# Tables of a state-space mixer set up in one batch, shorter norms, and two mixers' tails issued together, in a two-layer hybrid-head block

## The chip, the core and the metric

The kernel runs on one core of one Trainium2 chip. The metric is device time in microseconds of one execution; three runs are known, with a median of 4328.35 us (4321.64 to 4334.05). Lower is better.

## The reference, cut to what matters

Two layers act on 1024 latent tokens and 256 context tokens of width 1024, all in float32. Each layer modulates a norm, projects it, feeds four mixers of 256 channels each (gated linear attention, S5, Mamba2/SSD, latent attention), projects their outputs back and ends with a squared-ReLU MLP.

```python
def _modulate(h, g, shift, scale):
    return _rms(h, g) * (1.0 + scale) + shift

def s5_mixer(u_ctx, u_lat, a_re, a_im, log_step, b_re, b_im, c_re, c_im, d_skip, w_glu, b_glu):
    lam = lax.complex(a_re, a_im)
    lam_bar = jnp.exp(lam * jnp.exp(log_step)[..., None])
    b_bar = ((lam_bar - 1.0) / lam)[..., None] * lax.complex(b_re, b_im)
    ...
    h = scan(h -> lam_bar * h + b_bar u)        # forwards and backwards, 16 groups of 64 states
    y = real(c h) + d_skip * u
    y = gelu(y);  return y * sigmoid(y @ w_glu + b_glu)

for l in range(2):
    m = split(silu(c) @ w_mod[l] + b_mod[l], 6)
    a = _modulate(h, norm1_g[l], m[0], m[1]) @ w_in[l]
    ya, yb, yc, yd = gdn_mixer(a0), s5_mixer(a1), mamba2_mixer(a2), mla_mixer(a3)
    h = h + m[2] * (concat(ya, yb, yc, yd) @ w_out[l])
    h = h + m[5] * (relu(_modulate(h, norm2_g[l], m[3], m[4]) @ w_ff1[l])**2 @ w_ff2[l])
```

The S5 mixer needs tables of powers of `lam_bar` (magnitude, sine and cosine) for its chunks, which depend on the weights alone; the kernel makes them for both directions and 16 groups in each layer.

## The kernel before, in words

Tokens stand in three blocks of columns: block 0 (256 context tokens), blocks 1 and 2 (512 latent tokens each), always worked in the order 2, 0, 1, with features on the partitions. Every large product is made of three fp32r matmuls, high times high, low times high and high times low, so that each operand exists as a `hi` and a `lo` part: `a_hi` and `a_lo` for a normed block, `w_hi` and `w_lo` for a weight, `f_rh` and `f_rl` inside the ffn. The kernel is one list of instructions per engine: a scheduler written by hand (`Streams`) runs generators side by side by a virtual time, and each stage has a share (`SHARE`, line 147) that says how much virtual time its work costs. The list that comes out decides the order on each engine and on SP's DMA queue; nothing is reordered at run time.

The stages, by `main` (line 1823), with their times in the profile of before:

- Start, 0 to 69 us: the three blocks of `h` are loaded; `norm_scale` makes each block's scale (squares on ACT, sums `n_sq` and `n_acc` on DVE, a column sum on PE in `g`, `rsqrt` into `n_rr`, and a broadcast on PE that ACT copies to `n_acc`); `mod_pe` makes the first modulation vectors `md` and from them the gain `gs`; the stream `s5_tables` starts.
- Norms and the first part of the input projection to 325 us, its second part to about 650. `norm` (line 1633) makes for each of 8 pieces of 128 features `n_x`, then `a_hi` on ACT, then `n_x` once more and the difference `a_lo`. `norm_next` and `norm_all` chain the blocks: one starts when the one before is done.
- The mixers to 1310 us: SSD and latent attention (`mla`, names beginning with `m_`) in the main stream, and beside it the stream `beside`: linear attention (`gdn`, names beginning with `g_`), then S5 (names beginning with `5_`). S5 loads its parameters (`5_sd`, `5_wg`), its inputs (`5_U`), the block matrices `5_TZ` and 8 factor tables `5_fc`, does a recurrence, and ends with `s5_out`: gelu into `5_yf`, a gate product on PE, `5_mo`, and a store to the mixers' buffer `mx`.
- The output projection to 1404, the second norms, the ffn of layer 0 to 2440 us. Beside the ffn run layer 1's modulation vectors and from about 1870 us layer 1's S5 tables.
- Layer 1 in the same way: norms from 2404, mixers to 3474, second norms 3552 to 3625, ffn to 4309.

`s5_tables` (line 1205) calls `s5_setup` four times (two directions, two halves of 8 groups); each takes an exponential of the step, two exponentials of magnitude, and sines and cosines for 17 exponents (forms of 128x136). After each setup it calls `s5_products` four times: `5_t_hh` and `5_t_k` go through PE at once, then the co and si factors follow on DVE and POOL, and the result `5_fc` is stored to `s5d`. Both uses of `rsqrt` (line 268) are a bit trick and four Newton steps of four DVE instructions each. The inner part of `norm` reads

```python
x = self.t(wk, [128, 512], F32, "n_x", bufs=2)
nc.vector.tensor_tensor(x[:, :w], h[:, k], rb[:, :w], op=OP.mult)
nc.scalar.activation(hi[:, k], x[:, :w], AF.Identity, bias=sh, scale=gs)
```

and after it the second `n_x` is made in place, on ACT for odd pieces and on DVE for even ones; `a_lo` is on DVE for pieces 3 and 7 and on POOL for the other six. In `beside` the linear attention is finished, with its gating and its output stores (`outp`), before S5 begins.

## Time and profile before

| what | value |
|---|---|
| median of three runs | 4328.35 us (4321.64 to 4334.05) |
| the profiled execution, its own time | 4310.99 us |
| its span on the core | 4309.2 us |
| mean granted TensorE clock | 0.931 of full |
| PE busy | 3817.7 us, 89% of the span |
| DVE busy | 2716.2 us, 63% |
| POOL busy | 1455.5 us, 34% |
| ACT busy | 1259.1 us, 29% |
| DMA moved | 367.29 MB, 85 GB/s over the span |

The profile is of one execution. An engine is busy where one of its instructions ran; idle time is put down to what released the instruction behind it. In the rows all instructions carry line 125, a helper that issues them, so they are told apart by their tiles: `out<-in`, with an engine, an operation and a form. Names of tiles are those of the sections above; `mm`, `g`, `x`, `m` and `c` are accumulators in PSUM.

### The profile page before, as it was taken

How to read it: one execution, taken by the hardware profiler on the slowest of the kernel's cores; microseconds unless marked ns; L12 is line 12 of the kernel's file. 1: busy time of each engine (PE TensorE's matmuls, PEld its weight loads, DVE VectorE, ACT ScalarE, POOL GpSimd, SP SyncE). 2: the span in 40 equal slices, each digit the busy share in tenths (PEclk: the TensorE clock that was granted, in tenths of full speed). 3: DMA queues.
4: the chain of work that ended last, by engine and by line, in shares of the span. 5: the costliest groups of instructions: out<-in, count | busy, mean ns of one | idle time of the engine just before them, and what ended most of it. 6: DMA issues, size and time to landing. Idle time of an engine off the chain costs nothing.

```text
span 4309.2 us, 61386 instructions
## 1 busy us (share of the span) xinstructions
PE 3817.7 (89%) x23280; PEld 3058.1 (71%) x23280; DVE 2716.2 (63%) x6419; ACT 1259.1 (29%) x2015; POOL 1455.5 (34%) x1664
## 2 busy tenths in 40 slices
PE   5789897789978899999999798997959988999999
PEld 2567776667656688887788677775846676888887
DVE  7966567775644799997775645567765536444443
ACT  3324434333312411121222343244322323222121
POOL 3532533454451211133332224435435433222121
PEclk7899998789999999999999899998969999999999
DMA  5347520100345033311111243342041231111111
GB/s 184 125 159 221 194 98 32 45 2 5 74 123 176 30 98 98 103 60 55 50 62 62 81 136 100 106 144 76 14 106 52 58 135 32 57 40 59 40 59 59
DMA packets 170872, 367.29 MB, mean 85 GB/s; under 512 B 46160, under 2 KB 88400, under 8 KB 166864
## 3 DMA queue, kind: packets, MB, share of 16 engines
q1 hardware_dynamic: 170576, 363.37, 26.2%
q8 instruction: 183, 3.00, 0.3%
q14 instruction: 113, 0.93, 0.1%
HBM read 277.42 MB, written 85.89 MB: 84 GB/s over the span
## 4 chain that ended last, share of the span: by engine, by line
PE 46%; DVE 15%; POOL 3%; DMA 2%; ACT 2%; issue 2%; SPq 0%; DVEq 0%; ACTq 0%; POOLq 0%
PE mm L125 38%; PE m L125 3%; DVE mod_acc L125 3%; PE g L125 2%; PE c L125 2%; DVE h L125 2%; DVE n_x L125 1%; PE x L125 1%; DVE s_ca L125 1%; POOL a_lo L125 1%; POOL g_pr L125 1%; DVE g_scr L125 1%; DVE rsq_u L125 1%; SPq L125 0%; DVE f_r L125 0%
## 5 line engine op out<-in xcount | busy, mean ns | idle before, releaser
L125 PE MATMUL mm<-a_hi,w_hi 128*128 128x512 f32 (+1 forms) x2576 | 978.2, 381 | 45.5 <-ACT st L125 28.6
L125 PE MATMUL mm<-a_lo,w_hi 128*128 128x512 f32 (+1 forms) x2576 | 971.4, 378 | 38.0 <-POOL a_lo L125 18.5
L125 PE MATMUL mm<-a_hi,w_lo 128*128 128x512 f32 (+1 forms) x2576 | 965.8, 375 | 2.4 <-DVE w_lo L125 2.4
L125 POOL TENSOR_TENSOR w_lo<-w_raw,w_hi 128x1024 fp32r<-128x1024 f32 x189 | 465.0, 2469 | 1270.9 <-ACT w_hi L125 1268.9
L125 DVE SCALAR_TENSOR_TENSOR h<-mm,md,h 128x512 f32<-128x512 f32 (+1 forms) x680 | 467.4, 693 | 250.7 <-PE mm L125 246.9
L125 PEld LDWEIGHTS mm<-a_hi,w_hi 128*128 128x128 f32 x2576 | 499.1, 194 | 141.9 <-ACT st L125 32.6
L125 PEld LDWEIGHTS mm<-a_lo,w_hi 128*128 128x128 f32 x2576 | 500.4, 194 | 131.0 <-POOL a_lo L125 30.5
L125 PEld LDWEIGHTS mm<-a_hi,w_lo 128*128 128x128 f32 x2576 | 499.3, 194 | 83.9 <-DVE w_lo L125 2.9
L125 PE MATMUL mm<-f_rh,w_hi 128*128 128x512 f32 (+1 forms) x1280 | 478.3, 374 | 27.8 <-DVE f_r L125 13.7
L125 PE MATMUL mm<-f_rl,w_hi 128*128 128x512 f32 (+1 forms) x1280 | 473.6, 370 | 0.0
L125 PE MATMUL mm<-f_rh,w_lo 128*128 128x512 f32 (+1 forms) x1280 | 473.1, 370 | 0.0
L125 ACT CAST w_hi<-w_raw 128x1024 fp32r<-128x1024 f32 x234 | 242.2, 1048 | 735.5 <-PE mm L125 600.5
L125 DVE SCALAR_TENSOR_TENSOR f_r<-mm,f_r 128x512 f32<-128x512 f32 (+1 forms) x160 | 101.5, 634 | 360.1 <-ACT f_rh L125 359.4
L125 PEld LDWEIGHTS mm<-f_rh,w_hi 128*128 128x128 f32 x1280 | 243.7, 190 | 72.0 <-DVE h L125 16.5
L125 PEld LDWEIGHTS mm<-f_rh,w_lo 128*128 128x128 f32 x1280 | 243.1, 190 | 40.5
L125 PEld LDWEIGHTS mm<-f_rl,w_hi 128*128 128x128 f32 x1280 | 243.5, 190 | 39.1
L125 ACT ACTIVATE f_r<-mm 128x512 f32<-128x512 f32 (+1 forms) x160 | 88.1, 551 | 547.7 <-PE mm L125 474.0
L125 DVE SCALAR_TENSOR_TENSOR mod_acc<-mod_w,cond,mod_acc 128x128 f32<-128x128 f32 x672 | 240.4, 404 | 1.4
L125 POOL TENSOR_TENSOR m_sum<-m_sum,m_p 128x512 f32<-128x512 f32 x128 | 164.1, 1282 | 124.0 <-ACT m_p L125 117.9
L125 DVE SCALAR_TENSOR_TENSOR s_ca<-s_cx,s_prm,s_ca 128x255 f32<-128x255 f32 (+2 forms) x240 | 148.7, 644 | 24.4 <-ACT s_ca L125 22.1
L125 POOL TENSOR_TENSOR a_lo<-n_x,a_hi 128x512 fp32r<-128x512 f32 (+1 forms) x66 | 77.8, 1188 | 154.4 <-DVE n_x L125 139.5
L125 DVE TENSOR_TENSOR f_rl<-f_r,f_rh 128x512 fp32r<-128x512 f32 (+1 forms) x160 | 116.1, 726 | 2.0
(493 smaller groups left out, 6629.0 us busy)
## 6 DMA issues: line engine op xcount, KB each, us to landing
w_raw<-in_w_ff SPq DMA_DIRECT2D x128, 512.0 KB, 3.6
w_raw<-in_w_in SPq DMA_DIRECT2D x90, 512.0 KB, 3.9
mod_w<-in_w_mod SPq DMA_DIRECT2D x80, 512.0 KB, 3.7
pd<-st SPq DMA_DIRECT2D x80, 257.0 KB, 2.3
s5d<-5_fc SPq DMA_DIRECT2D x32, 577.0 KB, 2.8
5_fc<-s5d SPq DMA_DIRECT2D x16, 1154.0 KB, 6.3
g_cx<-pd SPq DMA_DIRECT2D x18, 643.0 KB, 4.9
h<-in_hT SPq DMA_DIRECT2D x4, 2048.0 KB, 9.9
```

The costliest lines, as they stand in the source:

```text
L125: return f(*args, **kw)
```

## The change

The first part batches the tables. A new `s5_small` makes the step's exponential, `xd`, `th`, the reduced angles `ph`, `rho` and the reciprocal `den` once for all 32 columns (16 groups, 2 directions); `s5_setup` takes its 8 columns of them. Sines, cosines and magnitudes are made for 9 exponents in place of 17 (forms of 128x72), and `s5_products` reads them reversed where it read the other 8. Its PE part goes behind the co and si factors, and its second operand has a buffer of its own, `5_t_o`. `5_prm` is loaded by 4 DMAs instead of 16, and the copy of `rho` goes from DVE to ACT. In the whole program DVE goes from 6421 to 5862 instructions, ACT from 2017 to 2048, POOL from 1669 to 1647, SP from 1023 to 1011; PE keeps 18658.

The second part shortens `rsqrt` to three Newton steps of three instructions (12 instead of 19 in all) and `norm` to a multiply by `gs` and the scale in one instruction. In 8 pieces DVE has 12 instructions of one kind where it had 8, 4 and 2 of three kinds; ACT keeps 12 and POOL has 4 `a_lo` in place of 6. `n_x` has 3 buffers.

The third part: at the start only block 2's scale is made ahead; blocks 0 and 1 make theirs in the chain of norms. `gdn` returns its last outputs as a generator, a pool `gx` is opened, and `beside` issues these outputs and S5 together; S5 loads `5_TZ` behind its first `5_fc`. Seven shares are new.

```diff
-SHARE = {"start": 1.4006, "norm": 7.9949, "mod": 0.7917, "tables": 3.0591, "conv": 0.1388, "ffn": 5.4917,
+SHARE = {"start": 2.8429, "norm": 7.0304, "mod": 0.7934, "tables": 2.7961, "conv": 0.1388, "ffn": 6.1066,
...
-        for k in range(4):
-            nc.vector.tensor_tensor(u, y, y, op=OP.mult)
+        for k in range(3):
+            nc.vector.scalar_tensor_tensor(u, y, -0.5, y, op0=OP.mult, op1=OP.mult)
             nc.vector.tensor_tensor(u, u, a, op=OP.mult)
-            nc.vector.tensor_scalar(u, u, -0.5, 1.5, op0=OP.mult, op1=OP.add)
-            o = out if (k == 3 and post == 1.0) else y
-            nc.vector.tensor_tensor(o, y, u, op=OP.mult)
+            o = out if (k == 2 and post == 1.0) else y
+            nc.vector.scalar_tensor_tensor(o, u, 1.5, y, op0=OP.add, op1=OP.mult)
...
-        with self.pool("gx", side) as p:
-            yield from outp(1, ot[1], p)
+        return lambda pool: outp(1, ot[1], pool)
...
         with self.pool("s5w", side) as ws:
+            sm = yield from self.s5_small(l, ws)
             for d in range(2):
                 for q in range(2):
                     tb = s5_views(self.t(ws, [128, TBW], F32, "5_tb"), S5_TB)
-                    yield from self.s5_setup(l, d, q, tb, ws)
+                    tb["rho"] = sm[5][:, 16 * d + 8 * q:16 * d + 8 * q + 8]
+                    yield from self.s5_setup(l, d, q, tb, ws, sm)
...
+        rev = lambda z: z[:, x, 7::-1] if d == 0 else z[:, x, 8:0:-1]
...
-            x = self.t(wk, [128, 512], F32, "n_x", bufs=2)
-            nc.vector.tensor_tensor(x[:, :w], h[:, k], rb[:, :w], op=OP.mult)
-            nc.scalar.activation(hi[:, k], x[:, :w], AF.Identity, bias=sh, scale=gs)
+            x = self.t(wk, [128, 512], F32, "n_x", bufs=3)
+            nc.vector.scalar_tensor_tensor(x[:, :w], h[:, k], gs, rb[:, :w], op0=OP.mult, op1=OP.mult)
+            nc.scalar.activation(hi[:, k], x[:, :w], AF.Identity, bias=sh)
             if k % 2:
-                nc.scalar.activation(x[:, :w], x[:, :w], AF.Identity, bias=sh, scale=gs)
+                nc.vector.scalar_tensor_tensor(lo[:, k], x[:, :w], sh, hi[:, k].bitcast(F32), op0=OP.add, op1=OP.subtract)
             else:
-                nc.vector.tensor_scalar(x[:, :w], x[:, :w], gs, sh, op0=OP.mult, op1=OP.add)
-            (nc.vector if k % 4 == 3 else nc.gpsimd).tensor_tensor(lo[:, k], x[:, :w], hi[:, k].bitcast(F32), op=OP.subtract)
+                nc.scalar.activation(x[:, :w], x[:, :w], AF.Identity, bias=sh)
+                nc.gpsimd.tensor_tensor(lo[:, k], x[:, :w], hi[:, k].bitcast(F32), op=OP.subtract)
...
-            yield [self.norm_scale(pn, h[i], "g", i, rb) for i in blocks] + [self.mod_pe(0, range(16), 4, 4, pm, ("mm", "mm"))]
+            yield [self.norm_scale(pn, h[2], "g", 2, rb), self.mod_pe(0, range(16), 4, 4, pm, ("mm", "mm"))]
...
-            norm_next(i, 0, 0, rb[i])
+            norm_next(i, 0, 0, rb.get(i))
...
-                yield from self.gdn(l, gP, put, G, tags, not last)
-                cm_o.__exit__(None, None, None)
-                yield from s5("right", ("m0", "c0", "m1", "c1"))
+                out = yield from self.gdn(l, gP, put, G, tags, not last)
+                cm_x, p = enter("gx", "right")
+                yield [out(p), s5("right", ("m0", "c0", "m1", "c1"))]
```

Three places of the order. The first is PE at the end of the start, before:

```order
11 L125 MATMUL mm<-ctab,mod_s 128x2 x4
12 L125 MATMUL mm<-mod_w,condp 32x512
13 L125 MATMUL g<-ctab,n_rr 128x128 x4
14 L125 MATMUL mm<-mod_w,condp 32x512 x7
15 L125 MATMUL mm<-ctab,mod_s 128x2 x4
16 L125 MATMUL g<-ctab,n_rr 128x128 x4
17 L125 MATMUL mm<-a_hi_837,w_hi 128x512 x2
18 L125 MATMUL g<-5_t_hh,5_tb 16x128
19 L125 MATMUL g<-ctab,5_t_k 128x128
```

and in the change:

```order
8 L123 MATMUL mm<-ctab,mod_s 128x2 x4
9 L123 MATMUL mm<-mod_w,condp 32x512 x8
10 L123 MATMUL g<-5_t_hh,5_tb 16x128
11 L123 MATMUL g<-ctab,5_t_o 128x128
12 L123 MATMUL g<-5_t_hh,5_tb 16x128
13 L123 MATMUL g<-ctab,5_t_o 128x128
14 L123 MATMUL mm<-ctab,mod_s 128x2 x4
15 L123 MATMUL g<-5_t_hh,5_tb 16x128
16 L123 MATMUL g<-ctab,5_t_o 128x128
17 L123 MATMUL g<-5_t_hh,5_tb 16x128
18 L123 MATMUL g<-ctab,5_t_o 128x128
19 L123 MATMUL mm<-a_hi_577,w_hi 128x512 x2
```

Here `mod_s` is the modulation's transpose, `n_rr` the scale's broadcast and `a_hi` the first gemm. The broadcasts of blocks 0 and 1 left this place, and four table products (a `5_t_hh` and a `5_t_o` each) are now ahead of the first gemm, two of them ahead of the last transposes. On DVE 221 instructions stood before the first `n_x` and 171 do now, and from there to block 1's last `a_lo` 184 and 112.

The second is SP's queue at the end of layer 0's mixers, before:

```order
290 L125 DMA g_cx_10913<-pd_7_102 128x1286
291 L125 DMA mx_7_0_160<-m_o 128x256
292 L125 DMA mx_1_0_142<-g_cx_10913 128x256
293 L125 DMA mx_1_1_143<-g_cx_10913 128x512
294 L125 DMA mx_1_2_144<-g_cx_10913 128x512
295 L125 DMA 5_sd<-in_s_db 128x4
296 L125 DMA 5_wg<-in_s_wg 128x2x256
297 L125 DMA 5_U<-ud_0_71 16x16x32 x8
298 L125 DMA 5_U<-ud_1_72 16x16x64 x8
299 L125 DMA 5_U<-ud_2_73 16x16x64 x8
300 L125 DMA 5_TZ<-s5k_69 16x16x128 x8
301 L125 DMA 5_fc<-s5d_67 128x2308
```

and in the change:

```order
290 L123 DMA g_cx_10615<-pd_7_102 128x1286
291 L123 DMA 5_sd<-in_s_db 128x4
292 L123 DMA 5_wg<-in_s_wg 128x2x256
293 L123 DMA 5_U<-ud_0_71 16x16x32 x8
294 L123 DMA 5_U<-ud_1_72 16x16x64 x8
295 L123 DMA 5_U<-ud_2_73 16x16x64 x8
296 L123 DMA 5_fc<-s5d_67 128x2308
297 L123 DMA 5_E_10659<-s5d_67 64x2x256 x2
298 L123 DMA 5_TZ<-s5k_69 16x16x128 x8
299 L123 DMA 5_fc<-s5d_67 128x2308
300 L123 DMA 5_E_10698<-s5d_67 64x2x256 x2
301 L123 DMA 5_fc<-s5d_67 128x2308
```

`g_cx` is the linear attention's gate, `mx_1` its outputs. S5's parameters and inputs now stand directly behind the gate's load, the outputs' stores behind the fifth factor table, and `5_TZ` behind the first. In layer 1 the same loads, and 4 of the 24 `5_U`, stand ahead of the loads for attention (`m_wq`, `m_P`) where they stood behind them.

The third is PE at the same place, where S5's last factor products end and its gate products begin, before:

```order
3510 L125 MATMUL c_11856<-5_p_11752,5_fc 128x160
3511 L125 MATMUL c_11856<-5_p_11753,5_E_11749 128x160
3512 L125 MATMUL x<-m_p,m_va 64x256
3513 L125 MATMUL x<-m_sum,ctab 64x256 x2
3514 L125 MATMUL m_11930<-5_yf,5_wg 128x512 x2
3515 L125 MATMUL c_11948<-5_yf,5_wg 128x512 x2
```

and in the change (the left-out rows are all attention's):

```order
3443 L123 MATMUL c_11374<-5_p_11277,5_E_11273 128x160
3444 L123 MATMUL g<-m_qhi,m_klo 128x256
3445 L123 MATMUL x<-m_p,m_va 64x256 x8
3446 L123 MATMUL mm<-m_qhi,m_khi 128x256
3447 L123 MATMUL mm<-m_qlo,m_khi 128x256
3448 L123 MATMUL mm<-m_qhi,m_klo 128x256
...
3508 L123 MATMUL mm<-m_qhi,m_klo 128x256
3509 L123 MATMUL x<-m_p,m_va 64x256 x8
3510 L123 MATMUL x<-m_sum,ctab 64x256 x2
3511 L123 MATMUL m_11464<-5_yf,5_wg 128x512 x2
```

Between the last `5_E` and the first `5_yf` there were 3 of attention's instructions, and there are 93.

## Rows read from the trace of the kernel before

**Rows 1.** The page, part 1: busy us and share of each engine.
```profile
PE 3817.7 (89%) x23280; PEld 3058.1 (71%) x23280; DVE 2716.2 (63%) x6419; ACT 1259.1 (29%) x2015; POOL 1455.5 (34%) x1664
```

**Rows 2.** Table by stretch, the start: busy us per engine, clock, DMA.
```profile
0.00:72.00 72.00, 30.95 (x133) 14.06 (x133) 47.97 (x240) 21.62 (x29) 15.64 (x27) 0.80 0.66 235
72.00:216.00 144.00, 101.08 (x403) 71.23 (x402) 128.26 (x347) 46.39 (x90) 80.44 (x105) 0.82 0.31 114
216.00:324.00 108.00, 93.25 (x606) 69.89 (x605) 64.59 (x193) 30.15 (x68) 40.78 (x77) 0.97 0.47 161
```

**Rows 3.** Table by stretch, the three later places with norms.
```profile
1404.00:1512.00 108.00, 84.75 (x409) 69.24 (x407) 84.93 (x196) 44.86 (x62) 34.99 (x24) 0.91 0.11 35
2376.00:2506.00 130.00, 99.67 (x483) 82.12 (x482) 82.19 (x173) 50.52 (x70) 32.25 (x33) 0.87 0.22 82
3540.00:3640.00 100.00, 79.78 (x322) 61.12 (x321) 61.03 (x112) 38.76 (x48) 30.05 (x18) 0.90 0.11 32
```

**Rows 4.** PE's waits, 60 to 320 us: total us, times, longest.
```profile
PE g L125 <- DVE 5_t_hh L125: 24.2, 8, 8.9
PE mm L125 <- POOL a_lo L125: 10.1, 7, 3.2
PE mm L125 <- DVE a_lo L125: 9.0, 4, 4.1
PE g L125 <- DVE 5_t_k L125: 5.1, 7, 1.7
PE g L125 <- DVE n_rr L125: 5.1, 1, 5.1
```

**Rows 5.** PE's waits, 1100 to 1316 us, layer 0's mixers.
```profile
PE m L125 <- ACT 5_yf L125: 30.6, 2, 19.1
```

**Rows 6.** PE's waits, 3100 to 3490 us, layer 1's mixers.
```profile
PE g L125 <- ACT m_kt L125: 16.0, 1, 16.0
```

**Rows 7.** DVE's timeline, the start: start us, us, instruction.
```profile
27.46 0.68 DVE L125 TENSOR_TENSOR n_sq<-n_sq 128x512 f32<-128x512 f32 x1
...
48.90 0.15 DVE L125 TENSOR_TENSOR rsq_u<-rsq_u,rsq_a 128x4 f32<-128x4 f32 x1
...
66.50 0.69 DVE L125 TENSOR_TENSOR n_x<-h,n_acc 128x512 f32<-128x512 f32 x1
```

**Rows 8.** DVE's timeline, one rsqrt alone, first and last instruction.
```profile
2482.45 0.16 DVE L125 TENSOR_SCALAR rsq_a<-g 128x4 f32<-128x4 f32 x1 [0.72 <-PE g L125]
...
2486.05 0.16 DVE L125 TENSOR_TENSOR n_rr<-rsq_y,rsq_u 128x4 f32<-128x4 f32 x1
```

**Rows 9.** Tile n_x, 2480 to 2510 us: ns min/median/max, starts.
```profile
L125 DVE TENSOR_TENSOR n_x<-h,n_acc x8: 676/692/1760, 2487.7 to 2501.4; 128x512 f32<-128x512 f32 x8
L125 ACT ACTIVATE a_hi<-n_x,md,gs x8: 802/815/819, 2488.4 to 2502.2; 128x512 fp32r<-128x512 f32 x8
L125 POOL TENSOR_TENSOR a_lo<-n_x,a_hi x6: 1268/1284/1296, 2489.9 to 2503.6; 128x512 fp32r<-128x512 f32 x6
```

**Rows 10.** PE's waits from 2376 to 2510 us.
```profile
PE g L125 <- DVE n_acc L125: 22.9, 4, 17.7
```

**Rows 11.** PE's groups, 1100 to 1316 us: busy us, mean ns.
```profile
L125 PE MATMUL x<-m_p,m_va 128*64 128x256 f32 x168 | 29.5, 401 | 0.0
L125 PE MATMUL mm<-m_qhi,m_khi 97*128 97x256 f32 x56 | 18.2, 324 | 0.7 <-ACT m_qhi L125 0.7
```

**Rows 12.** SP's timeline in layer 1's mixers.
```profile
3161.93 11.69 SPq L125 DMA_DIRECT2D 5_U<-ud  x24
```

**Rows 13.** DVE's groups, 1860 to 2376 us (layer 0's ffn).
```profile
L125 DVE SCALAR_TENSOR_TENSOR 5_ea_p<-5_ea_p,5_ea_r 128x8 f32<-128x8 f32 x48 | 16.3, 339 | 0.5
```

**Rows 14.** PE's waits from 1860 to 2376 us.
```profile
PE mm L125 <- DVE f_r L125: 13.7, 6, 6.8
PE mm L125 <- DVE h L125: 8.2, 2, 6.9
```

**Rows 15.** DVE's timeline, a pair of n_x in layer 0's last norms.
```profile
2434.98 4.49 DVE L125 TENSOR_TENSOR n_x<-h,n_acc 128x512 f32<-128x512 f32 x2 [0.75 <-POOL a_lo L125]
```

More of the change, by code (lines that the diff above doesn't have):

```diff
@@ L146 @@
 SIDE = 0.263
[L147 removed]
+SHARE = {"start": 2.8429, "norm": 7.0304, "mod": 0.7934, "tables": 2.7961, "conv": 0.1388, "ffn": 6.1066,
          "w1_0": 0.9376, "w2_0": 1.3776, "prep0_0": 0.1806, "solve0_0": 0.4513, "prep1_0": 0.4642,
          "solve1_0": 0.2102, "mla_0": 0.9476, "ssd_0": 0.8009, "s5_0": 1.3121, "w1_1": 0.7053, "w2_1": 0.9426,
[1 row of a table removed]
[L151 removed]
[1 row of a table added]
+         "ssd_1": 0.8561, "s5_1": 5.5532, "chain": 1.0205, "heads": 0.4024, "scan": 1.078, "factors": 2.0471}
 class Engines:
@@ L1265, in s5_products @@
             yield
+        b = self.bank(bk)
+        for g in range(2):
+            self.mm(b[0:16, 128 * g:128 * g + 128], bb[:, 0, x][:, g], E1[:, g, d:8 + d].rearrange("p s c -> p (s c)"))
+            self.tr(b[:, 256 + 128 * g:384 + 128 * g], ow[:, g].rearrange("p s c -> p (s c)"))
+        nc.scalar.copy(fc["E1"], E1[:, :, 1 - d:9 - d])
+        nc.scalar.copy(fc["rho"], tb["rho"][:, x])
+        K = self.t(ws, [16, 2, 8, 16], F32, "5_t_p")
+        K0 = self.t(ws, [16, 2, 16], F32, "5_K0")
+        if d == 1:
+            nc.sync.dma_start(K0, self.s5k[l][:, n, :, 7])
+        nc.scalar.copy(K, b[0:16, 0:256].rearrange("p (g s c) -> p g s c", g=2, s=8))
+        nc.scalar.copy(fc["Wo"], b[:, 256:512].rearrange("p (g x) -> p g x", g=2))
+        if d == 1:
+            nc.vector.tensor_tensor(K[:, :, 7], K[:, :, 7], K0, op=OP.add)
+        nc.sync.dma_start(self.s5k[l][:, n, :, 7 - 7 * d:15 - 7 * d], K)
+        yield
     def s5(self, l, put, bk, side="left", ctx_out=True, bufs=3):
@@ L1280, in s5 @@
                 TZ = self.t(wk, [128, 8, 2, 128], F32, "5_TZ")
-                for s in range(8):
-                    nc.sync.dma_start(TZ[16 * s:16 * s + 16], self.s5k[l][:, :, :, 7 - s:15 - s].rearrange("p n g s c -> p n g (s c)"))
                 def load(n):
@@ L1296, in factors @@
                         made[n] = load(n)
+                        for s in range(8) if n == 0 else ():
+                            nc.sync.dma_start(TZ[16 * s:16 * s + 16],
+                                              self.s5k[l][:, :, :, 7 - s:15 - s].rearrange("p n g s c -> p n g (s c)"))
                 def ins(n0):
@@ L1319, in s5_weights, with s5_small @@
         return sd, wg
-    def s5_setup(self, l, d, q, tb, ws):
+    def s5_small(self, l, ws):
+        nc, A = self.nc, self.A
+        self.mark("5_small")
+        prm = self.t(ws, [128, 3, 32], F32, "5_prm", bufs=1)
+        nc.sync.dma_start(prm[:, 0:2], A["s5_a"][l])
+        src = A["s5_ls"][l]
+        nc.sync.dma_start(prm[:, 2], bass.AP(tensor=src.tensor, offset=src.offset, ap=[[0, 128], [1, 32]]))
+        are, aim, dl = prm[:, 0], prm[:, 1], prm[:, 2]
+        self.exp_acc(ws, dl, dl, "5_ea")
+        xd, th, thr, rho, t8, den, w1 = [self.t(ws, [128, 32], F32, f"5_{n}", bufs=1)
+                                         for n in ("xd", "th", "thr", "rho", "t8", "den", "w1s")]
+        nc.vector.tensor_tensor(xd, are, dl, op=OP.mult)
+        nc.vector.tensor_tensor(th, aim, dl, op=OP.mult)
+        self.s5_reduce(ws, thr, th, None, "5_q")
+        yield
+        nc.vector.tensor_scalar(rho, xd, 8.0, None, op0=OP.mult)
+        self.exp_acc(ws, rho, rho, "5_ea")
+        yield
+        ph = self.t(ws, [128, 2, 32], F32, "5_ph", bufs=1)
+        nc.vector.tensor_scalar(t8, thr, 8.0, None, op0=OP.mult)
+        self.s5_reduce(ws, ph[:, 0], t8, None, "5_q")
+        nc.vector.tensor_scalar(t8, ph[:, 0], 16.0, None, op0=OP.mult)
+        self.s5_reduce(ws, ph[:, 1], t8, None, "5_q")
+        nc.vector.tensor_tensor(den, are, are, op=OP.mult)
+        nc.vector.tensor_tensor(w1, aim, aim, op=OP.mult)
+        nc.vector.tensor_tensor(den, den, w1, op=OP.add)
+        nc.vector.reciprocal(den, den)
+        yield
+        return are, aim, xd, thr, ph, rho, den
@@ L1340, in s5_setup @@
-        self.s5_reduce(ws, thr, th, None, "5_q")
-        yield
-        ex = bc(c["ex"][:, 17 * d:17 * d + 17], 1, NG)
+        are, aim, xd, thr = [z[:, gs] for z in sm[0:4]]
+        ph, den = sm[4][:, :, gs], sm[6][:, gs]
+        ex = bc(c["ex"][:, 9 * d:9 * d + 9], 1, NG)
         pre = tb["pre"]
@@ L1383, in s5_setup @@
         nc.vector.tensor_copy(ni, pim[:, :, m])
-        nc.vector.tensor_tensor(den, are, are, op=OP.mult)
-        nc.vector.tensor_tensor(w1, aim, aim, op=OP.mult)
-        nc.vector.tensor_tensor(den, den, w1, op=OP.add)
-        nc.vector.reciprocal(den, den)
         nc.vector.tensor_tensor(w1, nr, are, op=OP.mult)
```

67 lines of the change are left out of this document (15 added, 52 removed), and 2 rows, old and new, of the table SHARE.

## The prediction

> **What bounds the kernel now.** The page's first part comes first: PE is busy 89% of the span and no other engine over 63% [rows 1], so at most some 490 us lie outside PE's busy time and an edit on another engine pays only where PE waits for it. The second view is the table by stretch, which tells where that is. In the first 72 us PE is busy 31 us; from 72 to 216 us it is busy 101 of 144 us while DVE is busy 128; from 216 to 324 us it is at 93 of 108 [rows 2]. The stretches with norms in them leave PE idle 23, 30 and 20 us [rows 3]. The third view is PE's list of waits, which names the late ones: at the start the table products' operand `5_t_hh` (24.2 us) and `5_t_k`, then `a_lo` from POOL and DVE [rows 4]; at the end of layer 0's mixers the gate `5_yf` of the state-space mixer (30.6 us) [rows 5]; in layer 1's mixers the attention's `m_kt` [rows 6]. The granted clock is 0.80 and 0.82 where PE idles most, a mean between its two levels of 1.2 and 2.4 GHz, and 0.97 behind it [rows 2]; I add nothing for a higher clock, it is left in the range.
>
> **The start (term 1).** The first gemm stands behind `gs`, and the first `n_x` runs at 66.50 us [rows 7]. Before it 221 DVE instructions are in order, in the change 171. From 27.46 to 48.90 us DVE ran 116 instructions back to back, 0.18 us each [rows 7], so 50 fewer are 9 us; the modulation weights come over the same queue as before but now ahead of the table parameters, and block 2's scale is now made alone. I take 10 us. The other way, four table products now stand in PE's queue ahead of the last modulation transposes; they need `5_t_hh`, which is a few DVE rows earlier, so they cost about their own length.
>
> From the first `n_x` to block 1's last `a_lo` DVE goes from 184 to 112 instructions. DVE's 128 us in 72 to 216 us are 347 instructions, 0.37 us each [rows 2]; 72 fewer are 27 us of an engine that is nearly full there. Against this by waits: `5_t_hh` and `5_t_k` hold PE 29.3 us [rows 4]; the change puts the co and si factors ahead of the products' matmuls, so I count two thirds of it, 19 us, and a third of the 19 us for `a_lo`, 6 us. What is added is that blocks 0 and 1 now make their scale inside the norm chain: rsqrt, broadcast on PE, copy, first `n_x`, one after the other, about 6 us each for two blocks, as PE's wait for `n_rr` of 5.1 us now [rows 4]. By DVE's count the term is -10 - 27 = -37, by waits -10 - 19 - 6 + 12 = -23. I take **-30**; the ends are -5 (only the first wait goes, and the serial scales cost half of it) and -45.
>
> **The later norms (term 2).** One rsqrt alone runs from 2482.45 to 2486.21 us, 19 instructions of 0.20 us start to start [rows 8]; 12 remain, so 1.4 us a block. A block of 512 then takes from 2487.7 to 2505 us, 17 us for 8 pieces. DVE needs 0.69 us for an `n_x` alone, ACT 0.81 for each of its 12, POOL 1.28 for each of its 6 `a_lo` [rows 9]: none is full, the two buffers of `n_x` are, since each is held until POOL has read it. With three buffers and 4 POOL pieces in place of 6, ACT's 12 times 0.81 = 9.8 us is the longest engine, with hand-overs 11 to 12 us. So a stage of blocks 512, 256, 512 gets shorter by about 3 times 1.4, twice 5.5 and once 3, 18 us of chain. Three such stages lie beside idle times of 23, 30 and 20 us [rows 3], of which 17.7 in the largest is one wait for `n_acc` of the last block, at the end of that chain [rows 10]. I count somewhat under half of the idle: -9, -14 and -7, **-30**; the ends are -8 (only the rsqrts) and -50.
>
> **The mixers' tails (term 3).** In layer 0 between the state-space mixer's last factor matmul and its first gate matmul PE has 3 instructions of attention now and 93 in the change. The attention's two most frequent pieces cost 0.18 us (29.5 us by 168) and 0.32 us (18.2 by 56) [rows 11], so 93 are about 23 us of work at 0.25 each, put where PE waits 30.6 us for `5_yf` [rows 5]. The earlier start of that mixer is made by SP: its parameters and inputs stood behind the linear attention's output stores and no longer do. I take -16 of the 23, since the recurrence will share DVE and POOL with attention. In layer 1 the same edit meets `m_kt`, 16.0 us of wait [rows 6]: the 24 input transfers, 11.69 us on SP's queue [rows 12], now partly go ahead of the attention's loads, and some of them stay behind. I take -6. Together **-22**; the ends are +22 (11.69 us more for `m_kt` in layer 1, and as much in layer 0 where attention ends later) and -35.
>
> **The tables beside the ffn (term 4).** Layer 1's tables run beside layer 0's ffn. The exponential's 48 steps cost 16.3 us on DVE [rows 13]; they become a quarter in number, and the sine's steps about half as wide. PE waits there for `f_r` and `h`, 13.7 and 8.2 us [rows 14], both DVE's. A third goes: **-7**; ends 0 and -20.
>
> **The mixers' rsqrts (term 5).** Seven instructions of 0.20 us fewer in each; most lie beside PE's work of another mixer, and what hides them is that work. A few end a chain: **-4**; ends 0 and -8.
>
> **Sum.** -30 - 30 - 22 - 7 - 4 = -93 us, against the profiled execution's 4311: 4218. That execution is 17 us under the median, so 4235 against 4328, 2.1% faster. A measurement of this kernel can tell about 0.3%, 13 us, from no change. Not all ends come together; this case's own range is 4180 to 4280.
>
> **A rule that speaks against the change.** Every `n_x` and every odd `a_lo` becomes a DVE instruction with two inputs from SBUF, 12 in a block. `n_x`, a two-input instruction too, took 0.69 us on the median of a block, 1.76 at most, and a pair beside POOL's work 4.49 us, 2.25 each [rows 9, 15]. So some lengthen beside POOL; I kept the most of them at 0.69, and what the chain then is stands in term 2. The Trainium skill ("SBUF — State Buffer", section "Who interferes with whom") states that a DVE instruction with two SBUF inputs contends with a GpSimd instruction that reads SBUF, under an exclusive lock. The trace agrees as far as the 4.49 us pair beside the 0.69 us median goes; by that rule, with POOL reading all the time, the third rival below would be the result.
>
> **Rivals.** *Tails that give back (15%).* All else as above, but term 3 at +22: the loads of attention wait behind the inputs, and the state-space mixer runs slower beside it. For it: `m_kt` is layer 1's largest wait [rows 6]. Against: 30.6 us of empty PE in layer 0 have a filler in order. Sum -30 - 30 + 22 - 7 - 4 = -49: 4279.
>
> *DVE's relief is hidden (14%).* PE's own order decides and the norms' chains end as late: term 1 at -10 and term 2 at -8, the tails -22, the rest 0. Sum -40: 4288. For it: from 216 us on PE is at 93 of 108 us [rows 2]. Against: DVE is at 128 of 144 before.
>
> *The norms are blocked by POOL (9%).* Every one of the 12 two-input instructions takes 2.25 us, the pair's value [rows 15]. A block of 512 is then 27 us, against 17 now, and one of 256 some 5 us longer, +24 a stage, in four stages +96, if all of it is on the path. With the start's other parts (-10 - 19 + 12 = -17) and -22 - 7 - 4 it is +46: 4374, slower. The price decides above 17 / 12 = 1.4 us a piece; at 1.76 us, the longest single `n_x` of a block [rows 9], a stage is +9.5 and the sum near -12, no change. Against: POOL has 4 pieces where it had 6. Of its chance 6% are slower and 3% no change.
>
> **Chances.** The forecast has 62%, the rivals 15, 14 and 9. The first two rivals could each end a point lower, at no change. Faster by over 0.3%: 0.89, within 0.3%: 0.05, slower: 0.06. The range must reach over both milder rivals: 4185 to 4300. Under 4185 I leave some 7%, over 4300 some 12%.
>
> **What would show it.** Right: first `n_x` at 54 to 58 us; PE's wait for `5_t_hh` in the first 320 us under 10 us; a 512 block's norm in 11 to 13 us; `5_yf` in layer 0 under 15 us; the gain by the end of the first 330 us about 30, and 16 more at layer 0's output projection. Wrong: an `n_x` mean over 1.4 us, waits for `n_rr` over 12 us at the start, a wait for `m_kt` over 30 us, or a time before the mixers that is as long as now.

## The result, and the profile after

| what | before | after |
|---|---|---|
| median of four runs | 4325.23 us | 4248.93 us (4244.19 to 4252.79) |
| ratio after / before | | 0.982, 95% interval 0.980 to 0.984 |
| span of the profiled execution | 4309.2 us | 4245.2 us |
| PE / DVE busy | 3817.7 / 2716.2 us | 3808.6 / 2616.8 us |

The change makes the kernel 1.8% faster, 76 us by the medians and 64 us between the two profiled executions. It lies in the range, 14 us above the predicted time. PE's busy share goes from 89% [rows 1] to 90%; the page's first part of the changed kernel:

```profile
PE 3808.6 (90%) x23280; PEld 3065.8 (72%) x23280; DVE 2616.8 (62%) x5860; ACT 1244.5 (29%) x2046; POOL 1427.3 (34%) x1642
```

The time can be followed by a work that both kernels have in the same number and order: the 2576 matmuls `mm<-a_hi,w_hi` on PE. Their starts, read from PE's timeline (index from 0, us):

| index | place | before | after | difference | in the stage | forecast |
|---|---|---|---|---|---|---|
| 192 | in layer 0's input projection | 284.18 | 266.94 | -17.2 | -17.2 | -30 |
| 512 | near that projection's end | 601.87 | 591.45 | -10.4 | +6.8 | 0 |
| 576 | start of layer 0's output projection | 1346.40 | 1332.03 | -14.4 | -4.0 | -16 and a part of -4 |
| 832 | start of the ffn, after the second norms | 1597.78 | 1567.66 | -30.1 | -15.7 | -9 |
| 1472 | end of the ffn | 2404.15 | 2355.93 | -48.2 | -18.1 | -7 |
| 1600 | behind layer 1's first norms | 2549.33 | 2486.11 | -63.2 | -15.0 | -14 |
| 1984 | layer 1's output projection | 3516.09 | 3458.58 | -57.5 | +5.7 | -6 and a part of -4 |
| 2112 | behind layer 1's second norms | 3657.77 | 3594.19 | -63.6 | -6.1 | -7 |

From there to the last of these matmuls both kernels are equal to 0.01 us. The two profiled executions do not lie alike: that of the kernel before is 14 us under its median, that of the changed kernel 2 us, so the differences by stage add up to 64 us and not to 76. By this table the norms and the ffn gave more than forecast, the start about half, and the mixers' tails nothing. The table by stretch of the changed kernel, first the same three stretches as [rows 2], then the three norm stages of [rows 3], each moved with its stage:

```profile
0.00:72.00 72.00, 29.60 (x130) 15.34 (x131) 49.68 (x176) 21.62 (x35) 25.47 (x37) 0.76 0.71 257
72.00:216.00 144.00, 107.27 (x473) 79.77 (x472) 118.12 (x280) 47.38 (x104) 69.96 (x103) 0.81 0.33 121
216.00:324.00 108.00, 96.42 (x707) 72.34 (x705) 61.55 (x144) 35.95 (x79) 35.05 (x64) 0.95 0.55 186
1390.00:1498.00 108.00, 92.39 (x459) 76.50 (x458) 92.85 (x198) 43.31 (x66) 30.59 (x18) 0.94 0.14 44
2328.00:2458.00 130.00, 110.42 (x561) 92.69 (x560) 81.77 (x147) 52.17 (x79) 33.68 (x32) 0.92 0.35 128
3482.00:3582.00 100.00, 84.01 (x349) 65.95 (x348) 59.45 (x96) 37.59 (x50) 26.72 (x14) 0.93 0.10 32
```

By 216 us PE has done 603 matmuls where it had done 536, and the norm stages leave it idle 15.6, 19.6 and 16.0 us where it was 23, 30 and 20. PE's waits from 60 to 320 us, which answer to [rows 4]:

```profile
PE g L123 <- DVE 5_t_hh L123: 30.1, 5, 8.7
PE mm L123 <- POOL a_lo L123: 9.6, 5, 3.7
...
PE g L123 <- DVE n_rr L123: 2.5, 1, 2.5
...
PE mm L123 <- DVE a_lo L123: 1.0, 3, 0.4
```

The wait for `5_t_hh`, of which I expected less than 10 us, grew from 24.2 to 30.1 us. `5_t_k` and DVE's `a_lo`, 14.1 us together before, are all but gone (1.0 us). The waits at the end of layer 0's mixers, 1090 to 1332 us, answer to [rows 5]:

```profile
PE m L123 <- ACT 5_yf L123: 16.1, 2, 11.3
PE mm L123 <- ACT a_hi L123: 15.6, 1, 15.6
```

`5_yf` is halved, from 30.6 to 16.1 us, as 93 of attention's matmuls now stand there, but the wait for `a_hi`, the first operand of the output projection, is three times as long as in the kernel before, whose list from 1100 to 1346 us has

```profile
PE mm L125 <- ACT a_hi L125: 5.5, 2, 5.1
```

### The profile page after: what moved, and what is told of

Same layout as the page of the kernel before. It is cut to its first block, busy times and chain, and to the rows that moved or that the text cites. A ratio compares the mean times of both kernels' runs of the same rounds, so it can differ in the third digit from the quotient of the medians.

```text
span 4245.2 us, 60805 instructions
## 1 busy us (share of the span) xinstructions
PE 3808.6 (90%) x23280; PEld 3065.8 (72%) x23280; DVE 2616.8 (62%) x5860; ACT 1244.5 (29%) x2046; POOL 1427.3 (34%) x1642
## 4 chain that ended last, share of the span: by engine, by line
PE 63%; DVE 14%; POOL 5%; issue 3%; DMA 3%; ACT 2%; SPq 0%; ACTq 0%; POOLq 0%; DVEq 0%
PE mm L123 47%; PE m L123 6%; PE c L123 4%; PE g L123 3%; PE x L123 3%; DVE s_ca L123 1%; DVE g_scr L123 1%; DVE n_x L123 1%; DVE mod_acc L123 1%; POOL g_pr L123 1%; DMA s_cx<-pd 1%; DVE h L123 1%; POOL w_lo L123 1%; POOL m_sum L123 1%; DMA g_cx<-pd 1%
## 5 line engine op out<-in xcount | busy, mean ns | idle before, releaser
L123 PE MATMUL mm<-a_hi,w_hi 128*128 128x512 f32 (+1 forms) x2576 | 976.9, 380 | 43.0 <-ACT st L123 22.4
L123 POOL TENSOR_TENSOR g_bd<-sm_xt,ctab 64x512 fp32r<-64x512 f32 x76 | 82.8, 1102 | 81.1 <-PE c L123 43.1
```

What stands on the lines that cost most here:

```text
L123: return f(*args, **kw)
```

## The experiments

Each is the changed kernel with one part altered, unless said otherwise; ratios are to the kernel before, the changed kernel's being 0.982 (0.980 to 0.984).

**The loads of h behind the mixers' outputs.** SP's timeline of the changed kernel, then ACT's, show where the 15.6 us come from:

```profile
1286.38 0.59 SPq L123 DMA_DIRECT2D h<-in_hT  x1
1287.18 0.97 SPq L123 DMA_DIRECT2D mx<-5_mo  x2
1288.19 0.78 SPq L123 DMA_DIRECT2D h<-in_hT  x1
1289.06 9.95 SPq L123 DMA_DIRECT2D f_mx<-mx  x4
```
```profile
1301.32 2.63 ACT L123 CAST a_hi<-f_mx 128x512 fp32r<-128x512 f32 x4 [14.39 <-DMA f_mx<-mx]
```

Two loads of `h`, 2 MB and 1 MB, go out ahead of the first `f_mx`, and its data are there only at 1301.32 us, 12.3 us after its issue. S5's last two stores, issued among these loads, landed 10.1 us after their issue (1.7 before). In the kernel before the loads stood behind the `f_mx` (1310.53 issued, 1313.31 used, 2.8 us). It is so in every profile: 10.0 to 12.6 us in the eight kernels with the joined tail in layer 0 and the loads as in the changed kernel, 2.8 to 3.2 in the six others. The edit makes each load of `h` wait for the block's last `f_mx`:

```diff
                         h[i] = self.t(ph, [128, 8, w], F32, f"h{i}")
+                        nc.vector.tensor_copy(h[i][:, 0, 0:1], mx[:, 0:1])
                         nc.sync.dma_start(h[i], A["hT"][:, :, t0:t0 + w] if l == 0 else hd[i])
```

> The changed kernel, with layer reloads of h made to wait for the mixers' outputs (one column copied from the last f_mx of each block into h before its load). Theory: in layer 0 the gain of the joined tail is given back because two 2 MB and 1 MB loads of h go out ahead of the first f_mx load, which then takes 12.2 us where it took 2.8 before; behind f_mx it should take 3 to 5 us, PE's wait for a_hi there fall from 15.6 to 5 to 7 us, and the whole run be 8 to 10 us shorter (about 4240). Rival: the first gemm waits for the chain of S5's last outputs anyway, or for h itself in the first residual add: then under 3 us change.

Measured: 4232.40 us, ratio 0.9781 (0.9759 to 0.9802). The first `f_mx` is issued at 1274.99 and used at 1278.12 us, 3.1 us, and PE's waits from 1080 to 1332 us begin with

```profile
PE m L123 <- ACT 5_yf L123: 15.7, 2, 10.9
PE mm L123 <- ACT a_hi L123: 5.5, 1, 5.5
```

10.1 us of the wait for `a_hi` are gone: the theory holds. The other 6 us of the median are no effect of the edit that I can place (see the last section on the spread of equal work).

**All a_lo on DVE.** The part of the norm that stood on POOL and its second ACT pass are left out:

```diff
-            if k % 2:
-                nc.vector.scalar_tensor_tensor(lo[:, k], x[:, :w], sh, hi[:, k].bitcast(F32), op0=OP.add, op1=OP.subtract)
-            else:
-                nc.scalar.activation(x[:, :w], x[:, :w], AF.Identity, bias=sh)
-                nc.gpsimd.tensor_tensor(lo[:, k], x[:, :w], hi[:, k].bitcast(F32), op=OP.subtract)
+            nc.vector.scalar_tensor_tensor(lo[:, k], x[:, :w], sh, hi[:, k].bitcast(F32), op0=OP.add, op1=OP.subtract)
```

> The changed kernel with all eight a_lo of a norm on DVE in one instruction each, so that POOL and the second ACT pass have no part in a norm. Theory of contention: n_x and a_lo of 128x512 have a mean of 1.16 us because POOL's a_lo holds DVE, alone they need 0.74; then 16 instructions of 0.75 us are 12 us for a block where 12 of 1.16 are 14, and the run is 3 to 10 us shorter. Rival: the two-input form is slow by itself beside ACT and DMA; then the mean stays near 1.15, a block takes 18 us and the run is 10 to 20 us longer.

Measured: 4233.21 us, ratio 0.9783 (0.976 to 0.9807). It is 16 us faster than the changed kernel by the medians, with the ranges of the runs apart. The view of the tile `n_x` for the last block of 512 of layer 1's first norms in the changed kernel (ns min/median/max, first and last start), then the same block in this run:

```profile
L123 DVE SCALAR_TENSOR_TENSOR n_x<-h,gs,n_acc x8: 737/748/1875, 2424.4 to 2434.7; 128x512 f32<-128x512 f32 x8
L123 ACT ACTIVATE a_hi<-n_x,md x8: 707/723/727, 2425.2 to 2435.4; 128x512 fp32r<-128x512 f32 x8
...
L123 DVE SCALAR_TENSOR_TENSOR a_lo<-n_x,md,a_hi x4: 742/1162/2200, 2426.7 to 2436.2; 128x512 fp32r<-128x512 f32 x4
L123 POOL TENSOR_TENSOR a_lo<-n_x,a_hi x4: 1254/1298/1590, 2427.3 to 2436.6; 128x512 fp32r<-128x512 f32 x4
```
```profile
L123 DVE SCALAR_TENSOR_TENSOR n_x<-h,gs,n_acc x8: 743/743/750, 2404.8 to 2413.4; 128x512 f32<-128x512 f32 x8
...
L123 DVE SCALAR_TENSOR_TENSOR a_lo<-n_x,md,a_hi x8: 741/744/755, 2406.8 to 2414.9; 128x512 fp32r<-128x512 f32 x8
```

Beside POOL single instructions last up to 1.88 and 2.20 us; without POOL's part in the norm all 16 of this block lie between 0.741 and 0.755. The second ACT pass, which the edit also takes away, is not the cause: in the changed kernel's trace 43 of the 96 such DVE instructions of 128x512 overlap no POOL instruction, and they take 0.736 to 0.754 us, beside ACT or not, while each of the 33 that last over 0.8 us overlaps POOL for 0.67 us or more. The block takes 14 us in the changed kernel (2424.4 to the last `a_lo`, 2436.6 + 1.6) and 10.9 us here (2404.8 to 2414.9 + 0.75). By the matmul starts the stages with norms became 2.4 us (index 704 to 832), 5.9 us (1472 to 1600) and 3.6 us (2048 to 2112) shorter. That repeats: in the four kernels with all `a_lo` on DVE these stages take 157.9 to 160.3, 124.2 to 124.5 and 86.4 to 87.3 us, in the seven that differ from the changed kernel elsewhere or not at all 162.0 to 168.0, 129.7 to 131.5 and 90.0 to 90.8. Taking work away from the less busy engine and giving it to the busier one is the faster form here, since the first one stopped the other.

**S5 behind the linear attention's outputs again.**

```diff
-        return lambda pool: outp(1, ot[1], pool)
+        with self.pool("gx", side) as p:
+            yield from outp(1, ot[1], p)
...
-                out = yield from self.gdn(l, gP, put, G, tags, not last)
-                cm_x, p = enter("gx", "right")
-                yield [out(p), s5("right", ("m0", "c0", "m1", "c1"))]
-                for cm in (cm_x, cm_o):
-                    cm.__exit__(None, None, None)
+                yield from self.gdn(l, gP, put, G, tags, not last)
+                cm_o.__exit__(None, None, None)
+                yield from s5("right", ("m0", "c0", "m1", "c1"))
```

> The changed kernel with S5 again behind the linear attention's last outputs (the first factors still ahead of the block matrices). Theory: the join is worth little: first gemm of layer 0's output projection 4 us later against the start of the mixers, layer 1 equal within 5 us; the run within 8 us of the changed kernel. Rival, by my forecast of 22 us for the tails: 15 to 25 us longer.

Measured: 4242.90 us, ratio 0.9813 (0.9789 to 0.9838), no difference from the changed kernel that the intervals can tell. My 22 us for the tails are refuted for the change as it stands: the joined tail is worth nothing in sum. By the matmul starts it gains 7 us in layer 0's mixers (index 512 to 576 takes 748.0 us here, 740.6 in the changed kernel) and loses 13 in layer 1's (1664 to 1984: 906.5 and 919.7). S5's last output leaves at 1299.5 us here, where the joined tail has it at 1287.8, but the loads of `h` stand behind the first `f_mx` again, and the output projection starts at almost the same time, 1333.25 and 1332.03 us.

**The table stream slower.** One number: `"tables": 1.6` in place of 2.7961.

> The changed kernel with the share of the table stream at the start 1.6 in place of 2.8, so that the first table product stands 96 matmuls behind the first gemm instead of ahead of it and all are spread wider. Theory: at the start PE is held by table products placed earlier than DVE's chain can deliver them (waits for 5_t_hh of 34.1 us, three of 8 us at the first product of a setup); these waits fall under 12 us and the first gemm comes at 58 to 60 us, so 10 to 20 us shorter by the 192nd gemm step, of which some may be lost again where the linear attention waits for the tables. Rival: DVE is the limit of the start whatever PE's order is; then the waits move to a_lo and n_acc and the time stays within 5 us.

Measured: 4267.82 us, ratio 0.9861 (0.9839 to 0.9882), 19 us slower than the changed kernel. The matmul of index 192 starts at 239.12 us, 27.8 earlier than in the changed kernel, but that of index 576, the output projection, at 1345.77, 13.7 later. Between them the linear attention and S5 are on the path. In these kernels the linear attention's first instruction comes 1.5 to 4.2 us behind the store of the last table, which is at 275.4 us here, at 262.7 in the changed kernel and at 283.4 before (SP's timeline, the last `s5d<-5_fc`). S5's last output leaves at 1304.7, 1287.8 and 1310.2 us in the same order. The expectation on the waits failed too: PE's list from 60 to 320 us still has

```profile
PE g L123 <- DVE 5_t_hh L123: 30.1, 6, 8.8
```

PE waits as long for the products, with more of its own work done before. So in the first 300 us neither theory was right: what counts is not PE's lead, nor DVE's load as a whole, but when the table stream lets the linear attention start. Four other runs go the same way: with the last table at 263.6, 267.9, 268.0 and 285.4 us (old shares, old norm, old rsqrt, old tables) the output projection starts at 1331.9, 1336.4, 1344.1 and 1353.4. It is not the whole of it: with all `a_lo` on DVE it starts at 1318.2 after a last table at 263.1. The run with all three scales at the start, below, parts the end of the tables from the start of the linear attention.

**The old body of the norm.** The `norm` of the kernel before, with its two buffers, in the changed kernel.

> The changed kernel with the old body of the norm: a multiply, two scaled activations, six a_lo on POOL, two buffers of n_x. Theory: the new body is what shortened the three later norm stages (together 31 us between the two profiles); a block of 512 takes 17 us again where it takes 14, and the three stages are 20 to 28 us longer, the rest being rsqrt's; the run is 20 to 35 us longer. Rival: rsqrt and the shares made most of it; then under 10 us.

Measured: 4282.21 us, ratio 0.9895 (0.9873 to 0.9917), 33 us slower. The second norms of layer 0 (index 704 to 832) lose 11.2 us, layer 1's first (1472 to 1600) 5.3, layer 1's second (2048 to 2112) 3.8, all three outside what the seven profiles with the changed kernel's norm show. That is 20.3 us, as the theory says, of the 42.8 us between the two profiles; the execution profiled here was the slowest of its four. Another 10.3 are lost in the next 64 steps of layer 1's projection (63.1 us against 52.8). They are not shown to be the norm's: the kernel before, with the same body, takes 54.7 us there. The rest of the loss has no cause shown.

**The old shares of ffn and modulation.** `"ffn": 5.4917` and `"mod": 0.7917` again. (Eight shares differ between the two kernels, not seven as the section on the change has it; these are two of them.)

> The changed kernel with the old shares of the ffn and of the modulation stream, 5.49 and 0.792. Theory: the ffn of layer 0 became 20 us shorter, where I forecast 7, because the new share leaves DVE's queue freer for the ffn's own adds beside the modulation; with the old share 5 to 12 us of it are lost. Rival: the batched tables make all of it; then the ffn is within 2 us of the changed kernel's.

Measured: 4257.28 us, ratio 0.9843 (0.9817 to 0.987), which overlaps the changed kernel's; by the medians it is 8 us slower, and all four runs (4253.40 to 4273.46 us) lie above the changed kernel's. The profile says where it lies. In layer 0's ffn the stretch beside the modulation is 291 us in the kernel before and here, 284 in the changed kernel; with the old shares DVE has 804 instructions in it, with the new ones 710. In the table by stretch, of this run and then of the changed kernel:

```profile
1573.00:1864.00 291.00, 284.88 (x1533) 246.03 (x1532) 280.46 (x804) 52.54 (x82) 52.99 (x24) 0.99 0.29 94
1864.00:2373.00 509.00, 495.97 (x2545) 415.44 (x2544) 326.38 (x651) 108.73 (x213) 164.32 (x158) 0.98 0.17 57
```
```profile
1567.00:1851.00 284.00, 281.69 (x1526) 244.08 (x1525) 265.52 (x710) 51.40 (x79) 50.84 (x20) 1.00 0.30 95
1851.00:2356.00 505.00, 493.85 (x2561) 414.66 (x2560) 348.01 (x767) 110.38 (x217) 165.27 (x162) 0.99 0.18 59
```

Part of the 7 us is a part of the modulation moved behind, but not all is lost again there. By the matmul starts the whole ffn (index 832 to 1472) takes 799.5 us here, 806.4 in the kernel before, and 787.9 to 790.5 in the eleven profiles with the new shares and the new tables. So the old shares cost some 9 to 12 us, and the theory holds.

**The tables as before.** `s5_tables`, `s5_setup`, `s5_products`, the 17 exponents and the layout of `5_tb` of the kernel before, all else changed.

> The changed kernel with the tables as before: four setups with their own exponentials, 17 exponents, products' matmuls at once; all else changed. Theory: the tables' part is worth some 12 to 20 us in layer 0's ffn, and at the start it is worth what the linear attention gains when the last table is stored 10 to 20 us earlier; the run is 25 to 40 us longer. Rival: the tables are covered by other work in both places; then under 10 us.

Measured: 4313.58 us, ratio 0.9965 (0.9953 to 0.9978), 65 us slower than the changed kernel, more than the 25 to 40 expected. 21.4 us are lost by layer 0's output projection (index 576), where the last table is stored at 285.4 us instead of 262.7, and 35.2 in the ffn of layer 0 (index 832 to 1472). Its second part, where the tables stand, is 541 us long with PE busy 504, against 505 with 494 in the changed kernel and 516 with 494 before; PE's list of waits there begins

```profile
PE mm L125 <- DVE f_r L125: 18.3, 4, 8.8
PE mm L125 <- DVE h L125: 17.4, 6, 5.3
```

against 4.9 and 5.5 us in the changed kernel for the same two. The loss is larger than what the tables can have given in the change: under the old shares the ffn takes 806.4 us with the old tables (the kernel before) and 799.5 with the new ones (the run above), 6.9 us. I read the difference so: the new shares fit the shorter tables and let the old ones run into the ffn's own adds. So this run shows what the tables are worth under the new shares, and not a term of the sum.

**The old rsqrt.** Four steps of four instructions again.

> The changed kernel with the old rsqrt of 19 instructions. By my terms 1.4 us a block in the norms' chains, nine or ten of which end late, and 4 us in the mixers: 8 to 15 us longer. Rival: PE has other work in most of these places; under 4 us.

Measured: 4266.93 us, ratio 0.9857 (0.9834 to 0.988), 18 us slower. By the output projection of layer 0 it is 12.1 us behind the changed kernel, in layer 1's first norms it loses another 7.2 (index 1472 to 1600, PE's wait for `n_acc` there being 17.7 us against 13.4), and the rest is spread. Of the 12.1 us 5.4 are there by index 192, in the start, where the last table is stored at 268.0 us instead of 262.7; so at most some 7 can be the mixers', where I had 4, and single profiles do not tell that apart.

**All three scales at the start.** The line of `main` that makes the scales of blocks 2, 0 and 1 ahead is put back.

> The changed kernel with all three blocks' scales made ahead at the start, as before. Theory: the first gemm comes 5 to 8 us later, since the squares of two more blocks stand ahead of it on DVE, and two serial chains of 6 us are saved behind it: within 5 us of the changed kernel at layer 0's output projection. Rival: the serial chains are hidden and the first gemm's delay stays; 6 to 12 us longer.

Measured: 4247.81 us, ratio 0.9816 (0.9796 to 0.9836): no change. The first gemm starts 4.1 us later (67.85 us) and index 128 already 3.8 earlier. Theory and rival both miss the output projection, which starts 10.9 us earlier than in the changed kernel, and the run does not tell what the serial scales, 12 us of cost in my first term, cost, since more than the scales moved. The last table is stored late, about as in the kernel before, and still the linear attention is early: its loads and convolutions are in order beside the tables and not behind them. (Why they may stand there, though `beside` waits for `s5_tables` in the source, is not shown.) SP's timeline and ACT's here, then ACT's in the changed kernel, for the last table and the linear attention's first convolution:

```profile
280.98 0.34 SPq L123 DMA_DIRECT2D s5d<-5_fc  x1
```
```profile
205.21 1.36 ACT L123 ACTIVATE g_scr<-g_cx,g_cw 128x1282 f32<-128x1282 f32 x1
```
```profile
296.79 1.37 ACT L123 ACTIVATE g_scr<-g_cx,g_cw 128x1282 f32<-128x1282 f32 x1
```

S5's last output leaves at 1278.7 us, 9.1 earlier than in the changed kernel. The end of the tables is therefore no price by itself; it is one where the linear attention stands behind it. The lead is gone again by layer 1's output projection (0.8 us at index 1984), in stages with equal work.

**The three edits together, and the join by layer.** First all `a_lo` on DVE, `h` behind, and the join in layer 0 alone (in layer 1 the outputs come first); then the same with the join in both layers and in neither.

> The changed kernel with three edits: all a_lo on DVE, h's loads behind the mixers' outputs, and the joined tail in layer 0 alone. If the single gains add up (16 us from a_lo without POOL, 10 from the loads, some 10 from layer 1's tail) it is at 4210 to 4218. Rival: the join in layer 1 is not what costs, or the gains overlap: 4225 to 4235.

> The best version with the join in both layers (all a_lo on DVE, h's loads behind the mixers' outputs). Theory: the join costs some 5 to 10 us in layer 1, so 4220 to 4226 against 4216. Rival: layer 1 does not care; within 4 us.

> The same with the join in neither layer. Theory: with h's loads out of the way the join is worth 8 to 17 us in layer 0's tail, so 4224 to 4233. Rival: the tail of layer 0 is bound by the linear attention's own end and the join is worth nothing there; then 4214 to 4219.

| join | median us | range of its runs | ratio to before |
|---|---|---|---|
| layer 0 alone | 4215.80 | 4215.31 to 4220.68 | 0.9740 (0.9718 to 0.9761) |
| both layers | 4225.62 | 4216.78 to 4230.85 | 0.9760 (0.9738 to 0.9782) |
| neither | 4233.95 | 4228.43 to 4241.72 | 0.9782 (0.9760 to 0.9805) |

The first two expectations held, the third was missed by 1 us. The first is the best kernel, 2.6% faster than before and 33 us faster than the change. With the loads of `h` out of its way the join is worth 18 us in layer 0 (neither against layer 0 alone, ranges apart); that it costs 10 us in layer 1 is likely by the medians, but the ranges overlap. The stage itself speaks for it: from index 1664 to 1984 layer 1's mixers take 906.5 to 916.2 us in the four profiles without the join there and 915.5 to 925.8 in the ten with it, 9.5 us apart on the mean; between the best kernel and the one with both joins it is 2.8. So the sign is likely and the size open. PE's waits of the best kernel from 1070 to 1320 us show that layer 0's tail is still a chain:

```profile
PE m L123 <- ACT 5_yf L123: 15.4, 2, 10.6
PE mm L123 <- ACT a_hi L123: 5.8, 2, 5.5
PE c L123 <- DVE 5_xa L123: 3.6, 1, 3.6
PE m L123 <- POOL 5_p L123: 3.1, 1, 3.1
```

## Why the prediction was right in sum, and where its terms were not

**Term 1, the start: -30 forecast, -17 by index 192, -10 by index 512.** The step that failed is "I count two thirds of it, 19 us", the second summand of "by waits -10 - 19 - 6 + 12 = -23": the waits for table products were to shrink since their matmuls go behind the co and si factors. They did not shrink (`5_t_hh` and `5_t_k` 29.3 us before, `5_t_hh` alone 30.1 after): the first product of each setup still waits for that setup on DVE. Three waits of 8.2, 8.7 and 8.4 us, at 135.7, 182.7 and 227.8 us, in the changed kernel's PE timeline are 25 of the 30 us. And the price of the start is not PE's lead: the slower table stream gave PE 28 us by index 192 and lost them, with 14 more, in the mixers. What the start gave is that the linear attention, behind the tables in both kernels, could begin 23 us earlier (its first instruction is at 287.6 and 264.1 us). What of it arrived is seen in the run without the joined tail: S5's last output leaves 10.7 us and the output projection starts 13 us earlier than in the kernel before. This is one profile against another, and the rival "DVE's relief is hidden" had the term at -10. The first gemm came at 63.77, 5.8 us earlier, where I had 10; the first `n_x` started at 62.22, not at 54 to 58, as the last modulation transposes stood behind two table products, for whose `5_t_hh` PE waited 4.0 us. I had put these products at their own length.

**Term 2, the later norms: -30 forecast, -15.7, -15.0 and -6.1 measured, 37 in all** (the first stage holds the output projection's start as well). The mechanism was as told: in these three stages the old body costs 20.3 us and the old rsqrt some 10. Which part of the body gives it (the third buffer, the two pieces fewer on POOL, the shorter DVE work) was not tried. A block of 512 took 14 us where I had 11 to 13. The step that failed is "ACT's 12 times 0.81 = 9.8 us is the longest engine": it is DVE, with 27.1 us for two blocks, 13.6 each. The size of a piece was off in the direction of the rule that I had weighed: I kept the two-input instructions mostly at 0.69 us, and their mean over layer 1's first norms is 1.16. DVE's groups there in the changed kernel, 2340 to 2460 us, forms apart (busy us, mean ns, then idle time):

```profile
L123 DVE SCALAR_TENSOR_TENSOR n_x<-h,gs,n_acc 128x512 f32<-128x512 f32 x16 | 17.8, 1158 | 1.5 <-ACT n_acc L123 1.4
...
L123 DVE SCALAR_TENSOR_TENSOR a_lo<-n_x,md,a_hi 128x512 fp32r<-128x512 f32 x8 | 9.3, 1163 | 1.0 <-ACT a_hi L123 0.8
```

The third rival's mechanism was there at half its price, below the 1.4 us a piece from which it would have decided.

That is the place where the Trainium skill ("SBUF — State Buffer", section "Who interferes with whom") is borne out: it states that a DVE instruction with two SBUF inputs and a GpSimd instruction that reads SBUF exclude each other. The traces agree: beside no POOL instruction they take 0.736 to 0.754 us, and all that last over 0.8 us lie beside one. The barest case of it is a product of two tiles of 128x8, 0.15 us alone in other rows. DVE's and POOL's timelines of the changed kernel:

```profile
130.88 2.36 DVE L123 TENSOR_TENSOR 5_wi<-5_w,5_w 128x8 f32<-128x8 f32 x1
```
```profile
130.77 2.44 POOL L123 TENSOR_TENSOR w_lo<-w_raw,w_hi 128x1024 fp32r<-128x1024 f32 x1
```

It lasted 2.36 us, from 0.11 us after the start of POOL's `w_lo` to 0.03 us after its end.

**Term 3, the tails: -22 forecast, -4 and +5.7 measured with the mixers, and no difference when the join is undone.** The filler in the order was real: `5_yf` fell by 14.5 us (it is 32.7 again in the run without the join) and S5's last output left 22.4 us earlier (1310.2 to 1287.8 us), 11.7 of them by the join. The step that failed is "put where PE waits 30.6 us for `5_yf`", which ends the account at S5's gate and not at the output projection. Behind it stood a queue that I had not read: with the joined tail 3 MB of loads of `h` went ahead of the first `f_mx`, and PE's wait moved to `a_hi`. (That they may go earlier because the space of `h` is free earlier is my reading; the runs show the place alone.) The run with those loads behind shows it, and then layer 0's join is worth 18 us, near my 16. In layer 1 the forecast of -6 was wrong and the gain is probably a loss of some 9 us, as in the first rival, though not by `m_kt`, whose wait stayed (16.0 and 15.5 us); the wait for `m_sq`, attention's first operand, went from 5.3 to 14.8 us there.

**Term 4, the ffn of layer 0: -7 forecast, -18 measured.** The mechanism told gave what was forecast. Under the old shares of ffn and modulation the new tables are worth 6.9 us of the ffn (806.4 to 799.5), and there PE's waits for `f_r` and `h` beside the tables fall from 13.7 and 8.2 to 5.9 and 5.3 us, by half and not by a third. What I had put at nothing is the new shares: they give the other 11.2 us (799.5 to 788.3).

**Term 5, rsqrt in the mixers: -4 forecast.** The old rsqrt costs 18 us in all; some 10 of them are the norms' of term 2, 5.4 the start's, and what is left for the mixers is too small for single profiles to tell.

**The sum, and luck.** In the table of matmul starts terms 1, 3 and 5 gave 9 us where I had 56, and terms 2 and 4 gave 55 where I had 37. Against the profiled execution, from which the terms were taken, the sum is 29 us off: -93 forecast, -64 measured. That the gain by the medians, 76 us, lies 17 us from the forecast and not 29 is luck: the execution profiled before lay further under its kernel's median than the one profiled after.

**The rivals.** "DVE's relief is hidden" holds for the start, at its -10, and not for the norms. "Tails that give back" holds in part: layer 0's tail gave its gain back, by another queue than I named, and layer 1's mixers probably lost some. Neither holds for the whole.

## What to carry to other kernels

A gain on a path ends where the next queue begins: follow a shortened chain past its own last instruction, to every load that shares the DMA queue with its first consumer, and check what else now goes out ahead of it. In a kernel whose side stream sets a stage's end, a wait of the busiest engine is a price only if that engine's work is late there; date first when the side stream can start, and check whether what it stood behind still holds it. When two engines block each other, giving the less busy one a share can cost more than doing all of it on the busier one; measure one instruction alone and beside the other before splitting work between them.

## What the runs showed of the hardware that was not expected

Equal work in an equal order can vary by a larger share in one stage than the whole runs do. The changed kernel and the one with `h` behind have the same instructions in the same order up to the end of layer 0's mixers; from index 192 to 512 their profiles take 324.5 and 315.0 us, 3% apart where the runs of one kernel lie within 0.5%, with a granted clock of 0.97 and 0.93 in the one and 0.99 and 0.95 in the other (two stretches each). PE waits 25 and 21 us there, so 6 of the 9.5 us are matmuls at a lower mean of the two levels, 1.2 and 2.4 GHz. A difference of under some 10 us between two single profiles is therefore no evidence in such a stage. How far a stage repeats has to be read from the runs that share its work: the ffn, at a clock of 0.99 and 1.00, within 2.6 us over eleven profiles, the three norm stages within 6.0, 1.8 and 0.8 us over seven.

An ACT pass with a bias alone is shorter than one with a scale and a bias from columns: `a_hi` of 128x512 took 0.723 us on the median in the changed kernel and 0.815 before [rows 9]. The Trainium skill ("ScalarE: Activation LUTs", section "What ACT_TABLE_LOAD costs") states that each operand taken from a column adds about 93 ns; the 92 ns between the two rows agree.
